# A decoder trunk's opening in two token halves, with the first norm's factor applied after the in-projection

## The chip, the cores and the metric

The kernel runs on one core of one Trainium2 chip. The metric is the device time of one execution in microseconds (us); the median of several executions is given. A core has five engines that run side by side, each through its own queue in order: TensorE (PE; matrix products and transposes, writes PSUM), VectorE (DVE), ScalarE (ACT), GpSimd (POOL) and SyncE (SP; here it only issues DMA transfers). SBUF is the working memory of 128 partitions, PSUM the memory that PE writes to, in eight banks of 512 float32 values per partition.

## What is computed

Two layers over 512 tokens with 1024 features, float32. The change touches the start of layer 0, a Mamba-2 mixer:

```python
def rms_norm(x, g):
    y = x * lax.rsqrt(jnp.mean(x * x, axis=-1, keepdims=True) + EPS)
    return y * g

def mamba2_mixer(x, ln_g, in_w, conv_w, conv_b, dt_bias, a_log, ...):
    zxbcdt = rms_norm(x, ln_g) @ in_w              # 1024 -> 2048 + 3072 + 32
    z, xbc, dt = split(zxbcdt)
    xbc = silu(causal_dwconv(xbc, conv_w, conv_b)) # width 4, per channel
    xs, bm, cm = split(xbc)                        # 2048, 4 * 128, 4 * 128
    dt = softplus(dt + dt_bias)
    a = dt * (-exp(a_log))
    y = ssd_chunked(xs * dt, a, bm, cm) + xs * d_skip
    y = grouped_rms_norm(y * silu(z))              # 4 groups
    return y @ out_w

x = x + mamba2_mixer(x, ...)
x = x + conv_ffn(x, ...)
# layer 1: differential attention with shared K/V, then conv_ffn
```

The norm's factor `rsqrt(mean(x^2) + EPS)` is one number per token, `g` one number per feature. Since the in-projection sums over features, the factor may be applied to x or to each token's result.

## The kernel before

Activations lie feature-major: a tile holds 128 features (partitions) by 512 tokens. x is eight such tiles `xT[k]` (the residual, tile `xTt`). Every product runs in split precision: an operand is rounded to the fast format (`xgh`, `wh`), the rest is kept as a second operand (`xgl`, `wl`), and three matmuls make one product (`mm3`: wh·xh, wh·xl, wl·xh). A block of 128 output features over 1024 input features is 24 matmuls of 512 columns.

Weights stream through `emit_chunk`: a DMA of 512 KB on SP's queue into one of three `raw` buffers, then `wh` on ACT (L148) and `wl` on DVE (L149). `plan` lists the chunks in the order of use, and `chunk(key)` emits up to two ahead. The tile framework allots buffers and writes semaphore waits; a scheduler places instructions on each engine's queue by its estimates, except those that `tc.keep_in_program_order` pins.

The opening (pool `ph0`): SP loads four blocks of 128 tokens by 1024 features (`xt`, L221), then the dt weights (128 KB) and the first weight chunks. ACT loads the convolution's parameters and the norm's `g` into `st1`. PE runs ten fp32 and eighteen fast warming matmuls (L257, L260) and turns `st1` into `c1`. For each token block ACT squares and sums (L267) and takes the root (L268), DVE inverts it (L269) and multiplies the block by it (L270) into `xr`. PE turns `xr` into eight PSUM banks, one per k (`xgt`, L274); each bank gets two readers, ACT's `xgh[k]` (times g, L277) and DVE's `xgl[k]` (L278). Then follow the dt product (16 matmuls, L435 and L439), block in32 (group 0's B), the four transposes of dt (L446), block in36 (group 0's C), and in16 to in19 (its x). From dt, DVE computes softplus and `A`, and PE the cumulated decays (`ps_dec`); two tables go to DRAM and come back broadcast as `m` and `er` (POOL's DMA queue, `fetch`).

Each of four groups then runs: two blocks for B and C and four for x, each with a width-4 convolution (`conv_block`: ACT takes the first tap from PSUM, DVE the other three, ACT applies SiLU); the chunked scan of four chunks (`scan`: `tokens`, `masked`, `states`, `outputs`), woven with the four z blocks (`z_blocks`: SiLU on ACT from PSUM); then `xs * z`, squares, their sum (`gacc`, L678), the group's norm factor (`tr_g`, `al_g`), and the out-projection of the group before, which adds to the residual `xT`.

The residual itself is not kept from the opening. In group 1 the same four blocks of x are loaded again (`x0` to `x3` in `plan`), turned by PE (32 transposes, L307) and copied to `xT` by ACT (L308), one block after each convolution block (`stream_in`).

Of the kernel before, what the change touches and what calls it, by code (L numbers as in the profile page):

```python
# [39 lines left out]
def trunk_kernel(ctx: ExitStack, tc, x, ssm_ln_g, ssm_in_w, ssm_conv_w, ssm_conv_b, ssm_dt_bias,  # L40
# [19 lines left out]
    def aux_bank(name):  # L60
        return pp.tile([P, T], F32, tag="aux", name=name)
# [60 lines left out]
    def emit_chunk():  # L122
# [5 lines left out]
        if key[0] == "x":  # L128
            raw = wrp.tile([P, D], F32, tag="raw", name="wr_" + key)
            sync.dma_start(raw, src)  # L130
            ready.append((key, raw, None))
            return
        nk, ncol = plan[i][2:4]
        n = nk * ncol
        raw = wrp.tile([P, 1024], F32, tag="raw", name="wr_" + key)
        wh = wp.tile([P, 1024], F32R, tag="wh", name="wh_" + key)
        wl = wp.tile([P, 1024], F32R, tag="wl", name="wl_" + key)
        sync.dma_start(raw[:, :n].rearrange("p (k c) -> p k c", k=nk), src)
        if len(plan[i]) > 4:

            for k in range(nk):
                ks = slice(k * ncol, (k + 1) * ncol)
                g = c2[:, plan[i][4] + k:plan[i][4] + k + 1]
                act.activation(wh[:, ks], raw[:, ks], AF.Copy, scale=g)
                dve.scalar_tensor_tensor(out=wl[:, ks], in0=raw[:, ks], scalar=g,
                                         in1=wh[:, ks].bitcast(F32), op0=ALU.mult, op1=ALU.subtract)
        else:
            act.activation(wh[:, :n], raw[:, :n], AF.Copy)  # L148
            dve.tensor_tensor(out=wl[:, :n], in0=raw[:, :n], in1=wh[:, :n].bitcast(F32), op=ALU.subtract)  # L149
        ready.append((key, wh[:, :n].rearrange("p (k c) -> p k c", k=nk),  # L150
                      wl[:, :n].rearrange("p (k c) -> p k c", k=nk)))

    def dt_chunk():

        key, src, nk, ncol = plan[0]
        state["next"] = state["use"] = 1
        raw = wrp.tile([P, 1024], F32, tag="raw", name="wr_dt")
        w = wp.tile([P, 1024], F32R, tag="wh", name="w_dt")
        rv = raw[:, :nk * ncol].rearrange("p (k c) -> p k c", k=nk)
        wv = w[:, :2 * nk * ncol].rearrange("p (k j c) -> p k j c", k=nk, j=2)  # L160
        sync.dma_start(rv, src)
        act.activation(wv[:, :, 0, :], rv, AF.Copy)
        dve.tensor_tensor(out=wv[:, :, 1, :], in0=rv, in1=wv[:, :, 0, :].bitcast(F32), op=ALU.subtract)
        return wv
# [26 lines left out]
    eps_c = cp.tile([P, 1], F32, name="eps_c")  # L191
    dve.memset(eps_c, EPS)
# [24 lines left out]
    with tc.tile_pool(name="ph0", bufs=1) as p0:  # L217
        xt = [p0.tile([P, D], F32, name="xt%d" % b) for b in range(NT)]
        xr = [p0.tile([P, D], F32, name="xr%d" % b) for b in range(NT)]
        for b in range(NT):  # L220
            sync.dma_start(xt[b], x[0, b * P:(b + 1) * P, :])  # L221
        st1 = p0.tile([P, P], F32, name="st1")
        act.preload_act_table_set("sqrt_and_others")
        act.dma_start(st1[0:96, :], ssm_conv_w.rearrange("o k (b p) -> (o k b) p", p=P))
        act.dma_start(st1[96:120, :], ssm_conv_b.rearrange("o (b p) -> (o b) p", p=P))
        act.dma_start(st1[120:128, :], ssm_ln_g.rearrange("o (b p) -> (o b) p", p=P))
        act.dma_start(dtb, ssm_dt_bias[0].partition_broadcast(P))
        act.dma_start(alog, ssm_a_log[0].partition_broadcast(P))
# [23 lines left out]
        wst = [p0.tile([P, P], F32R, name="wst%d" % i) for i in range(2)]  # L252
        wmv = p0.tile([P, T], F32R, name="wmv")
        for t in (*wst, wmv):
            dve.memset(t.bitcast(F32), 0.5)
# [6 lines left out]
        pe.transpose(ps[:, :P], st1, ident)  # L262
        dve.tensor_copy(c1, ps[:, :P])
        ss = p0.tile([P, NT], F32, name="ss")
        rs = p0.tile([P, NT], F32, name="rs")
        for b in range(NT):
            act.activation(xr[b], xt[b], AF.Square, accum_out=ss[:, b:b + 1])  # L267
            act.activation(rs[:, b:b + 1], ss[:, b:b + 1], AF.Sqrt, bias=eps_c, scale=1.0 / D)  # L268
            dve.reciprocal(rs[:, b:b + 1], rs[:, b:b + 1])  # L269
            dve.tensor_scalar(out=xr[b], in0=xt[b], scalar1=rs[:, b:b + 1], scalar2=None, op0=ALU.mult)  # L270
        pss = [(mm_bank if k % 2 else aux_bank)("xgt%d" % k) for k in range(KB)]
        for b in range(NT):
            for k in range(KB):
                pe.transpose(pss[k][:, b * P:(b + 1) * P], xr[b][:, k * P:(k + 1) * P], ident)  # L274
        for k in range(KB):
            g = c1[:, 120 + k:121 + k]
            act.activation(xgh[k], pss[k], AF.Copy, scale=g)  # L277
            dve.scalar_tensor_tensor(out=xgl[k], in0=pss[k], scalar=g, in1=xgh[k].bitcast(F32),  # L278
                                     op0=ALU.mult, op1=ALU.subtract)

    def params_a():
        dve.tensor_copy(st2[64:80, :].rearrange("p (j q) -> p j q", j=2),
                        d2[64:80, :].unsqueeze(2).to_broadcast([16, 2, 64]))
# [5 lines left out]
    def params_b():  # L289
# [4 lines left out]
        dve.tensor_tensor(out=lamv[:, 0], in0=lamv[:, 0], in1=lamv[:, 1], op=ALU.mult)  # L294
        dve.tensor_tensor(out=lamv[:, 1], in0=lamv[:, 2], in1=lamv[:, 3], op=ALU.mult)
        dve.reduce_sum(le, lamv[:, 0:2], axis=AX.X)
        act.activation(le, le, AF.Exp)
# [3 lines left out]

    def stream_in(b):
        xb, _ = chunk("x%d" % b)
        for q in range(2):
            ps = aux_bank("xt%d_%d" % (b, q))
            for k in range(4):
                pe.transpose(ps[:, k * P:(k + 1) * P], xb[:, (4 * q + k) * P:(4 * q + k + 1) * P], ident)  # L307
            act.activation(xTt[:, 4 * q:4 * q + 4, b * P:(b + 1) * P],  # L308
                           ps.rearrange("p (k t) -> p k t", k=4), AF.Copy)
# [47 lines left out]
    def along_tokens(r, name):  # L357

        ps = aux_bank("al_" + name)
        for b in range(NT):  # L360
            pe.transpose(ps[:, b * P:(b + 1) * P], r[:, 2 * b:2 * b + 1].to_broadcast([P, P]), ident)
        return ps
# [50 lines left out]
    with tc.tile_pool(name="ssm_y", bufs=1) as yp, tc.tile_pool(name="ssm", bufs=1) as sp:  # L413
        def in_block(key):
            wh, wl = chunk(key)
            ps = mm_bank("ps_" + key)
            for k in range(KB):
                mm3(ps, wh[:, k, :], wl[:, k, :], xgh[k], xgl[k], k == 0, k == KB - 1)
            return ps

        def conv_block(j, key, dst):
            ps = in_block(key)
            w = lambda t: c1[:, t * 24 + j:t * 24 + j + 1]
            tmp = sp.tile([P, T], F32, tag="ctmp", name="ctmp%d" % j, bufs=2)
            act.activation(tmp, ps, AF.Identity, bias=c1[:, 96 + j:97 + j], scale=w(3))
            for s in range(1, 4):
                dve.scalar_tensor_tensor(out=tmp[:, s:], in0=ps[:, :T - s], scalar=w(3 - s),
# [4 lines left out]
        wdt = dt_chunk()  # L432
        ps = aux_bank("ps_dt")
        for k in range(KB):
            both = lambda: pe.matmul(ps[:2 * NH, :], wdt[:, k].rearrange("p j c -> p (j c)"), xgh[k],  # L435
                                     start=(k == 0), stop=(k == KB - 1))
            if k < KB - 1:
                both()
            pe.matmul(ps[:NH, :], wdt[:, k, 0, :], xgl[k], start=False, stop=False)  # L439
            if k == KB - 1:  # L440
                both()
        dtT = sp.tile([P, T], F32, tag="ctmp", name="dtT", bufs=2)[:2 * NH, :]
        act.activation(dtT, ps[:2 * NH, :], AF.Copy)
# [11 lines left out]
        dve.tensor_tensor(out=v4(dt), in0=pv[:, :, 1, :], in1=v4(dt), op=ALU.add)  # L455
        dve.tensor_tensor(out=v4(dt), in0=v4(dt),
# [45 lines left out]
        class Chunk:  # L502
# [11 lines left out]
            def fetch(self):  # L514
# [4 lines left out]
                if self.c:  # L519
                    self.er = sp.tile([P, 4, P], F32, tag="er", name="er" + self.tag, bufs=3)  # L520
# [85 lines left out]
        def z_blocks(g, zs):  # L606
            for b in range(4):
                ps = in_block("in%d" % (4 * g + b))
                z = sp.tile([P, T], F32, tag="z", name="z%d_%d" % (g, b), bufs=4)
                act.activation(z, ps, AF.Silu)  # L610
# [38 lines left out]
        for g in range(NG):  # L649
# [6 lines left out]
            conv_block(16 + g, "in%d" % (32 + g), bT)  # L656
# [4 lines left out]
            for b in range(4):  # L661
# [3 lines left out]
                if g == 1:  # L665
                    stream_in(b)
# [343 lines left out]
```

## Time and profile before

| | us |
|---|---|
| median of 3 runs | 1390.85 (1390.69 to 1392.38) |
| the profiled execution | 1389.46 |
| its span, first to last instruction | 1387.6 |
| PE busy in the span | 1367.3 |
| DVE busy | 893.6 |
| ACT busy | 671.5 |
| granted clock of PE, mean | 0.999 |

The profile is of one execution. In a row of the timeline the first number is the start in us, the second the length, then engine, line, operation and tiles (out <- in), and in brackets the idle time of the engine just before it, with what ended it. A row of groups (by line) ends with busy time, the mean of one in ns, and idle time before. A row of waits names the waiting engine, tile and line, what it waited for, and the total, the number and the longest. A row of windows gives the stretch, its length, the busy time of each engine, PE's granted clock (1.00 is full), the DMA share and GB/s. A busy PE is not PE at its peak: matmuls of 512 columns last 0.39 us each but follow each other every 0.23 us.

### The profile page before, as it was taken

How to read it: one execution, taken by the hardware profiler on the slowest of the kernel's cores; microseconds unless marked ns; L12 is line 12 of the kernel's file. 1: busy time of each engine (PE TensorE's matmuls, PEld its weight loads, DVE VectorE, ACT ScalarE, POOL GpSimd, SP SyncE). 2: the span in 40 equal slices, each digit the busy share in tenths (PEclk: the TensorE clock that was granted, in tenths of full speed). 3: DMA queues.
4: the chain of work that ended last, by engine and by line, in shares of the span. 5: the costliest groups of instructions: out<-in, count | busy, mean ns of one | idle time of the engine just before them, and what ended most of it. 6: DMA issues, size and time to landing. Idle time of an engine off the chain costs nothing.

```text
span 1387.6 us, 17001 instructions
## 1 busy us (share of the span) xinstructions
PE 1367.3 (99%) x6480; PEld 1105.0 (80%) x6480; DVE 893.6 (64%) x1481; ACT 671.5 (48%) x1108; POOL 93.2 (7%) x117
## 2 busy tenths in 40 slices
PE   8999999999999999999999999999999999999998
PEld 6777787787878888888888786786778888888886
DVE  6687767768677775357754546748687774367741
ACT  6785644742344443134433557757654442144431
POOL 4330300300020000000001000000020000000000
PEclk9999999999999999999999999999999999999999
DMA  6655433432223333233323422221133332333322
GB/s 183 163 148 148 129 91 107 129 103 65 80 88 107 91 97 101 91 104 95 93 82 112 114 90 68 66 87 39 48 103 93 93 105 91 99 99 91 99 92 69
DMA packets 188422, 137.18 MB, mean 99 GB/s; under 512 B 6852, under 2 KB 177268, under 8 KB 188340
## 3 DMA queue, kind: packets, MB, share of 16 engines
q1 hardware_dynamic: 181312, 122.93, 30.1%
q0 software_dynamic: 4400, 12.01, 2.9%
q10 hardware_dynamic: 2628, 1.15, 0.3%
q8 instruction: 51, 0.84, 0.2%
q14 instruction: 31, 0.25, 0.1%
HBM read 133.82 MB, written 2.25 MB: 98 GB/s over the span
## 4 chain that ended last, share of the span: by engine, by line
PE 76%; DVE 5%; ACT 4%; issue 1%; DMA 0%; POOL 0%; POOLq 0%; ACTq 0%
PE ps_u L175 6%; PE ps_u L177 6%; PE ps_d L176 6%; PE ps_d L177 6%; PE ps_u L176 6%; PE ps_d L175 6%; PE ps_g L176 6%; PE ps_g L177 6%; PE ps_g L175 5%; PE ps_in L175 2%; PE ps_in L177 2%; PE ps_in L176 2%; PE ps_o L176 2%; PE ps_o L177 2%; PE ps_o L175 1%
## 5 line engine op out<-in xcount | busy, mean ns | idle before, releaser
L176 PE MATMUL ps_g<-xgl,wh_g 128*128 128x512 f32 x352 | 137.2, 390 | 1.5 <-DVE xgl L319 1.5
L175 PE MATMUL ps_d<-hh,wh_d 128*128 128x512 f32 x352 | 137.5, 391 | 0.0
L177 PE MATMUL ps_d<-hh,wl_d 128*128 128x512 f32 x352 | 137.2, 390 | 0.0
L175 PE MATMUL ps_u<-xgh,wh_u 128*128 128x512 f32 x352 | 137.1, 390 | 0.0
L176 PE MATMUL ps_u<-xgl,wh_u 128*128 128x512 f32 x352 | 137.1, 390 | 0.0
L175 PE MATMUL ps_g<-xgh,wh_g 128*128 128x512 f32 x352 | 137.0, 389 | 0.1
L176 PE MATMUL ps_d<-hl,wh_d 128*128 128x512 f32 x352 | 137.0, 389 | 0.0
L177 PE MATMUL ps_u<-xgh,wl_u 128*128 128x512 f32 x352 | 136.9, 389 | 0.0
L177 PE MATMUL ps_g<-xgh,wl_g 128*128 128x512 f32 x352 | 136.9, 389 | 0.0
L175 PE MATMUL ps_in<-xgh,wh_in 128*128 128x512 f32 x320 | 126.9, 397 | 0.0
L177 PE MATMUL ps_in<-xgh,wl_in 128*128 128x512 f32 x320 | 126.3, 395 | 0.0
L176 PE MATMUL ps_in<-xgl,wh_in 128*128 128x512 f32 x320 | 125.9, 393 | 0.0
L149 DVE TENSOR_TENSOR wl_d<-wr_d,wh_d 128x1024 fp32r<-128x1024 f32 (+1 forms) x48 | 54.5, 1136 | 91.7 <-ACT wh_d L148 91.5
L148 ACT ACTIVATE wh_d<-wr_d 128x1024 fp32r<-128x1024 f32 (+1 forms) x48 | 47.5, 990 | 129.5 <-PE ps_d L176 115.3
L724 ACT ACTIVATE hh<-vg 128x512 fp32r<-128x512 f32 x44 | 27.8, 631 | 114.9 <-DVE vg L723 114.9
L707 DVE TENSOR_TENSOR uu<-ps_u,nr_f 128x512 f32<-128x512 f32 x44 | 30.4, 692 | 79.6 <-PE ps_u L177 79.6
L176 PEld LDWEIGHTS ps_g<-xgl,wh_g 128*128 128x128 f32 x352 | 66.1, 188 | 16.0 <-DVE xgl L319 2.3
L175 PEld LDWEIGHTS ps_g<-xgh,wh_g 128*128 128x128 f32 x352 | 66.1, 188 | 14.2 <-ACT xgh L318 0.5
L177 PEld LDWEIGHTS ps_u<-xgh,wl_u 128*128 128x128 f32 x352 | 66.1, 188 | 13.7
L176 PEld LDWEIGHTS ps_u<-xgl,wh_u 128*128 128x128 f32 x352 | 66.1, 188 | 13.7
L176 PEld LDWEIGHTS ps_d<-hl,wh_d 128*128 128x128 f32 x352 | 66.1, 188 | 13.6
L177 PEld LDWEIGHTS ps_d<-hh,wl_d 128*128 128x128 f32 x352 | 66.1, 188 | 13.5
(315 smaller groups left out, 2950.4 us busy)
## 6 DMA issues: line engine op xcount, KB each, us to landing
wr_g<-in_ffn_up_w_dram SPq DMA_DIRECT2D x44, 512.0 KB, 3.8
wr_u<-in_ffn_up_w_dram SPq DMA_DIRECT2D x44, 512.0 KB, 3.9
wr_in<-in_ssm_in_w_dram SPq DMA_DIRECT2D x40, 512.0 KB, 3.9
wr_d<-in_ffn_down_w_dram SPq DMA_DIRECT2D x40, 512.0 KB, 3.5
m<-cumd POOLq DMA_DIRECT2D x16, 512.0 KB, 5.1
wr_out<-in_ssm_out_w_dram SPq DMA_DIRECT2D x16, 512.0 KB, 3.4
wr_k<-in_kv_w_dram SPq DMA_DIRECT2D x8, 512.0 KB, 3.9
wr_q<-in_q_w_dram SPq DMA_DIRECT2D x8, 512.0 KB, 4.1
```

The lines of the kernel that those rows point to most:

```text
L148: act.activation(wh[:, :n], raw[:, :n], AF.Copy)
L149: dve.tensor_tensor(out=wl[:, :n], in0=raw[:, :n], in1=wh[:, :n].bitcast(F32), op=ALU.subtract)
L175: pe.matmul(ps, wh, xh, start=start, stop=False)
L176: pe.matmul(ps, wh, xl, start=False, stop=False)
L177: pe.matmul(ps, wl, xh, start=False, stop=stop)
L707: dve.tensor_tensor(out=u, in0=ps, in1=r, op=ALU.mult)
L724: act.activation(h, ga, AF.Copy)
```

## The change

- The opening works in halves of 256 tokens. x is turned as it is, without the norm's factor. A PSUM bank (`xgt0_q`, `xgt1_q`) holds two k slices of one half.
- SP issues x0, x1, the dt weights, in32's weights, x2, x3. ACT loads only `g` (`st0`, turned into `g1`) and the convolution's weights; POOL loads its bias, `dtb` and `alog`.
- For half 0 and then half 1: ACT and DVE make `xgh` and `xgl` (times g) for 256 tokens, PE runs the dt product and block in32 over those columns. The order on the engines is pinned.
- The residual is copied from the same PSUM banks (`keep`), two of half 0's on DVE early, the rest later on DVE and ACT; the second load of x, its turns and copies in group 1 are gone.
- Sums of squares go to `rs`, for x0 and x2, x3 on ACT and x1 on DVE. The inverse root is computed on DVE by `rsqrt` (twelve small steps). PE spreads it along tokens (`al_x`), ACT copies it to `nr_x`.
- Each block of the in-projection is multiplied by `nr_x` on DVE, before the convolution (`u`) and before z's SiLU; dt is multiplied by `rs`.
- The table of functions that ACT loads first is another; the eighteen fast warming matmuls are gone; `er` has two buffers in place of three.

```diff
@@ plan
-            if g == 1:
-                plan.append(("x%d" % b, x[0, b * P:(b + 1) * P, :]))
@@ opening
-        for b in range(NT):
+        for b in range(2):
             sync.dma_start(xt[b], x[0, b * P:(b + 1) * P, :])
-        act.preload_act_table_set("sqrt_and_others")
+        act.dma_start(st0, ssm_ln_g.rearrange("o (b p) -> (o b) p", p=P))
+        act.preload_act_table_set("natural_log_exp_and_others")
...
-        for n in (T, T // 2, P):
-            for i in range(6):
-                pe.matmul(warm[:, :n], wst[i % 2], wmv[:, :n], start=True, stop=True)
...
+        def turn(h, b, q):
+            for k in range(2):
+                pin(pe.transpose(pv[h][q][:, k, (b % 2) * P:(b % 2 + 1) * P],
+                                 xt[b][:, (2 * q + k) * P:(2 * q + k + 1) * P], ident))
+
+        def high(h, m):
+            pin(act.activation(xgh[m][:, half[h]], pv[h][m // 2][:, m % 2], AF.Copy, scale=g1[:, m:m + 1]))
+
+        def low(h, m):
+            pin(dve.scalar_tensor_tensor(out=xgl[m][:, half[h]], in0=pv[h][m // 2][:, m % 2],
+                                         scalar=g1[:, m:m + 1], in1=xgh[m][:, half[h]].bitcast(F32),
+                                         op0=ALU.mult, op1=ALU.subtract))
+
+        def keep(h, q, on):
+            o = xTt[:, 2 * q:2 * q + 2, half[h]]
+            pin(act.activation(o, pv[h][q], AF.Copy) if on is act else dve.tensor_copy(o, pv[h][q]))
...
+        half = (slice(0, 256), slice(256, T))
+        pst = [[aux_bank("xgt0_%d" % q) for q in range(4)]]
+        pv = [[p.rearrange("p (k t) -> p k t", k=2) for p in pst[0]]]
+        pin(act.activation(sq[0], xt[0], AF.Square, accum_out=rs[:, 0:1]))
+        pin(dve.tensor_tensor_reduce(sq[1], xt[1], xt[1], 1.0, 0.0, ALU.mult, ALU.add, rs[:, 1:2]))
+        wdt = dt_chunk()
+        for b in range(2):
+            for q in range(4):
+                turn(0, b, q)
+        for m in range(KB):
+            high(0, m)
+            low(0, m)
+            if m in (1, 3):
+                keep(0, m // 2, dve)
+            if m == 3:
+                emit_chunk(pin)
+                for b in range(2, NT):
+                    sync.dma_start(xt[b], x[0, b * P:(b + 1) * P, :])
+        wb0 = ready[0][1:]
+        ps_dt, ps_b0 = mm_bank("ps_dt"), mm_bank("ps_in32")
+        dt_part(half[0])
+        pst.append([(mm_bank if q < 2 else aux_bank)("xgt1_%d" % q) for q in range(4)])
+        pv.append([p.rearrange("p (k t) -> p k t", k=2) for p in pst[1]])
+        turn(1, 2, 0)
+        turn(1, 2, 1)
+        b0_part(half[0])
+        turn(1, 2, 2)
+        turn(1, 2, 3)
+        for q in range(4):
+            turn(1, 3, q)
+        for m in range(KB):
+            high(1, m)
+            low(1, m)
+        dt_part(half[1])
+        b0_part(half[1])
+        emit_chunk(pin)
+        for q in range(2, 4):
+            keep(0, q, dve)
+        for q in range(4):
+            keep(1, q, act)
+        emit_chunk(pin)
+        chunk("in32")
+        for b in (2, 3):
+            pin(act.activation(sq[0], xt[b], AF.Square, accum_out=rs[:, b:b + 1]))
@@ conv_block, z_blocks
+            u = sp.tile([P, T], F32, tag="u", name="u%d" % j, bufs=2)
+            dve.tensor_tensor(out=u, in0=ps, in1=rr, op=ALU.mult)
...
-            act.activation(tmp, ps, AF.Identity, bias=c1[:, 96 + j:97 + j], scale=w(3))
+            act.activation(tmp, u, AF.Identity, bias=c1[:, 96 + j:97 + j], scale=w(3))
...
-                act.activation(z, ps, AF.Silu)
+                dve.tensor_tensor(out=z, in0=ps, in1=rr, op=ALU.mult)
+                act.activation(z, z, AF.Silu)
@@ the norm's factor, dt
+        rsqrt(rs, sp, "x", [P, NT], D)
+        rr = bp.tile([P, T], F32, tag="nr", name="nr_x")
+        act.activation(rr, along_tokens(rs, "x", 1), AF.Copy)
...
+        dve.tensor_tensor(out=v4(dt), in0=v4(dt), in1=rs.unsqueeze(2).to_broadcast([P, NT, NH]), op=ALU.mult)
@@ er
-                    self.er = sp.tile([P, 4, P], F32, tag="er", name="er" + self.tag, bufs=3)
+                    self.er = sp.tile([P, 4, P], F32, tag="er", name="er" + self.tag, bufs=2)
```

`dt_part(ts)` and `b0_part(ts)` are the 16 matmuls of the dt product and the 24 of block in32 over the columns `ts`; in `b0_part` the low weights come last.

More of the change, by code (lines that the diff above doesn't have):

```diff
@@ L127, in emit_chunk @@
         key, src = plan[i][:2]
[L128 to L132, printed above, removed]
         nk, ncol = plan[i][2:4]
@@ L263, in trunk_kernel @@
[L263 to L270, printed above, removed]
@@ L271, in trunk_kernel @@
-        pss = [(mm_bank if k % 2 else aux_bank)("xgt%d" % k) for k in range(KB)]
-        for b in range(NT):
-            for k in range(KB):
[L274 to L279, printed above, removed]
+        pe.transpose(ps[:, :KB], st0, ident[:KB, :KB])
@@ new lines, in trunk_kernel @@
+        dve.tensor_copy(g1, ps[:, :KB])
+        sq = [p0.tile([P, D], F32, name="xsq%d" % i) for i in range(2)]
+        def turn(h, b, q):
[8 more added lines that the diff above has]
+                                         op0=ALU.mult, op1=ALU.subtract))
@@ new lines, in keep, with dt_part @@
+        def keep(h, q, on):
+            o = xTt[:, 2 * q:2 * q + 2, half[h]]
+            pin(act.activation(o, pv[h][q], AF.Copy) if on is act else dve.tensor_copy(o, pv[h][q]))
+        def dt_part(ts):
+            for k in range(KB):
+                both = lambda: pin(pe.matmul(ps_dt[:2 * NH, ts], wdt[:, k].rearrange("p j c -> p (j c)"),
+                                             xgh[k][:, ts], start=(k == 0), stop=(k == KB - 1)))
+                if k < KB - 1:
+                    both()
+                pin(pe.matmul(ps_dt[:NH, ts], wdt[:, k, 0, :], xgl[k][:, ts], start=False, stop=False))
+                if k == KB - 1:
+                    both()
@@ new lines, in b0_part @@
+        def b0_part(ts):
+            for k in range(KB):
+                pin(pe.matmul(ps_b0[:, ts], wb0[0][:, k, :], xgh[k][:, ts], start=k == 0, stop=False))
+                pin(pe.matmul(ps_b0[:, ts], wb0[0][:, k, :], xgl[k][:, ts], start=False, stop=False))
+            for k in range(KB):
+                pin(pe.matmul(ps_b0[:, ts], wb0[1][:, k, :], xgh[k][:, ts], start=False, stop=k == KB - 1))
+        half = (slice(0, 256), slice(256, T))
+        pst = [[aux_bank("xgt0_%d" % q) for q in range(4)]]
@@ L413, in trunk_kernel, with in_part @@
     with tc.tile_pool(name="ssm_y", bufs=1) as yp, tc.tile_pool(name="ssm", bufs=1) as sp:
+        def in_part(ps, wh, wl, ts):
+            for k in range(KB):
+                mm3(ps[:, ts], wh[:, k, :], wl[:, k, :], xgh[k][:, ts], xgl[k][:, ts], k == 0, k == KB - 1)
         def in_block(key):
```

85 lines of the change are left out of this document (33 added, 52 removed).

## Prediction

> **What bounds the kernel now.** I read the page's part 1 first, then the list of waits of PE, then the opening as a timeline, then windows of busy time in the stretch where the change also works.
>
> ```profile
> span 1387.6 us, 17001 instructions
> PE 1367.3 (99%) x6480; PEld 1105.0 (80%) x6480; DVE 893.6 (64%) x1481; ACT 671.5 (48%) x1108; POOL 93.2 (7%) x117
> PE tr_g L351 <- DVE gacc L678: 2.5, 2, 1.3
> PE xgt L274 <- DVE xr L270: 1.6, 2, 1.2
> PE ps_dt L435 <- DVE xgl L278: 1.6, 1, 1.6
> PE cb L539 <- ACT xT L308: 1.2, 1, 1.2
> ```
>
> PE is busy 1367.3 of 1387.6 us; all its idle time is 20.3 us. So a change can win PE work that it takes out, one of these waits, or opening time in which PE runs things that lead nowhere. This kernel's end is PE's end: I follow when PE finishes a block, before and after.
>
> ```profile
> 0.81 4.58 SPq L221 DMA_DIRECT2D xt<-in_x_dram  x4
> 5.07 1.06 ACT L267 ACTIVATE xr<-xt 128x1024 f32<-128x1024 f32 x1 [2.98 <-DMA xt<-in_x_dram]
> 6.03 0.19 ACT L267 ACTIVATION_READ_ACCUMULATOR xr<-xt 128x1 f32 x1
> 6.27 1.06 ACT L267 ACTIVATE xr<-xt 128x1024 f32<-128x1024 f32 x1
> 10.80 1.06 ACT L267 ACTIVATE xr<-xt 128x1024 f32<-128x1024 f32 x1 [1.65 <-DMA xt<-in_x_dram]
> 11.86 0.40 ACT L162 ACTIVATE w_dt<-wr_dt 128x256 fp32r<-128x256 f32 x1
> 13.26 1.06 ACT L148 ACTIVATE wh_in<-wr_in 128x1024 fp32r<-128x1024 f32 x1 [0.81 <-DMA wr_in<-in_ssm_in_w_dram]
> 14.22 4.72 ACT L277 ACTIVATE xgh<-xgt,c 128x512 fp32r<-128x512 f32 x8
> 16.29 0.45 PE L435 MATMUL ps_dt<-xgh,w_dt 128*64 128x512 f32 x1 [1.56 <-DVE xgl L278]
> 26.15 0.39 PE L175 MATMUL ps_in<-xgh,wh_in 128*128 128x512 f32 x1
> 31.59 0.39 PE L175 MATMUL ps_in<-xgh,wh_in 128*128 128x512 f32 x1
> ```
>
> This is the opening: first number the start, second the length, in brackets the idle time and who ended it. The first token block of x is there at 5.07, the fourth at 10.80; only then are the eight conversions xgh possible (14.22), the dt product starts at 16.29, and PE then runs without a gap: dt, in32, four small transposes, from 26.15 in36, from 31.59 in16. So 31.59 is the mark: everything up to in36, with dt turned, is done.
>
> **The change, part by part.** First what is taken out. In group 1 x is read again, turned by PE and copied by ACT.
>
> ```profile
> L307 PE MATMUL xt<-ident,wr_x x32: 270/272/273, 109.2 to 129.0; 128*128 128x128 f32 x32
> L308 ACT ACTIVATE xT<-xt x8: 584/592/601, 111.2 to 131.5; 128x512 f32<-128x512 f32 x8
> 128.25 1.04 PE L307 MATMUL xt<-ident,wr_x 128*128 128x128 f32 x8
> 129.13 0.49 PE L548 MATMUL xs<-ident,xs 128*128 128x128 f32 x3
> 131.65 0.49 PE L539 MATMUL cb<-cT,bT 128*128 128x128 f32 x2 [1.24 <-ACT xT L308]
> ```
>
> The 32 turns come in groups of eight, and one group holds PE from 128.25 to 129.13, 0.88 us; four make 3.5. The copies sit on ACT, and the last holds a PSUM bank for which PE waits 1.24. Four loads leave SP's queue, no load is late there. Gain 3.5 + 1.24 = 4.75 us. If something else is late at 131.65, up to 1.24 of it stays: 3.5 to 4.75. I take 4.75. Also gone are the 18 warming matmuls, the fp32 factor multiplies xr and square roots of the opening; the first were in front of PE's wait and hide nothing, the others are replaced below.
>
> Now the new opening. SP issues x0, x1, the dt weights, in32, x2, x3, and POOL takes over three small loads from ACT's queue ahead of its own, whose results are used far later. x0 and x1 are there at 5.07 and 6.27 (rows above), turned by 7.3. The dt weights, queued behind all of x, were used at 11.86; now two blocks of x fewer stand before them, at 1.2 us each and some weight traffic moved back: 7.2 to 8.2. I start the first conversion at 7.95. Its length for 256 columns is not in the trace; neighbours are
>
> ```profile
> L277 ACT ACTIVATE xgh<-xgt,c 128x512 fp32r<-128x512 f32 x8 | 4.7, 699 | 0.0
> L278 DVE SCALAR_TENSOR_TENSOR xgl<-xgt,c,xgh 128x512 fp32r<-128x512 f32 x8 | 5.4, 742 | 0.0
> L149 DVE TENSOR_TENSOR wl_in<-wr_in,wh_in 128x1024 fp32r<-128x1024 f32 x5 | 6.1, 1220 | 1.7 <-ACT wh_in L148 1.6
> L458 DVE SCALAR_TENSOR_TENSOR sp_p<-dt 128x128 f32<-128x128 f32 x1 | 0.3, 291 | 0.0
> 359.03 0.17 DVE L326 TENSOR_SCALAR rsm_g<-tr_g 128x8 f32<-128x8 f32 x1
> 359.24 0.17 DVE L327 TENSOR_SCALAR tr_g<-rsm_g 128x8 int32<-128x8 int32 x1
> ```
>
> ACT: 0.40 for 256 columns from SBUF with a constant factor (w_dt), 0.70 for 512 from PSUM with a column factor, so 0.40 to 0.60; I take 0.50. DVE: 0.29 at 128, 0.74 at 512, on the line between them 0.44. I add 0.05 for each hop.
>
> What decides is the bank. A half of 256 tokens puts two k slices into one PSUM bank, and in the new program's waits the engines take the bank in turns: xgh of the odd slice waits for xgl of the even one. Before, each k had a bank of its own, so ACT ran ahead. A bank now costs 0.50 + 0.05 + 0.44 + 0.05, twice, = 2.08; the even xgh of the next bank overlaps, so each further one adds 1.53. Four banks: 2.08 + 3 x 1.53 = 6.7 us per half, where the full width took DVE's 5.4. In the first half DVE also copies two banks to the residual (0.6 each, as ACT's L308) and makes in32's low part (1.22, waiting for ACT's 1.06): I add 2.4, and the half ends at 7.95 + 6.7 + 2.4 = 17.0.
>
> PE is in order: behind dt's first half come four turns (0.44), in32's first half (24 matmuls of 256 columns at a pitch of half of 0.23, 2.9), then the turns that the second half's first conversion needs (0.7). So that starts at 17.3 + 0.44 + 2.9 + 0.7 = 21.4, ends at 28.1; dt's last matmul 28.4, in32's second half 31.3, and in36 starts at 31.4 against 26.15.
>
> Before in36 can end, PE must turn the norm's factor rs (four transposes), and the squares of x2 and x3 were put late on ACT: after the last xgh at 27.6 come wh_in36 1.06, four residual copies 2.4, wh_in16 1.06, square 1.25, wh_in17 1.06, square 1.25 = 35.7. DVE's twelve small steps of the inverse root have a pitch of 0.20 (rows L326, L327): 38.1. PE has done in36's first 23 matmuls at 31.4 + 5.2 = 36.6 and waits 1.5. Four transposes, four for dt, one matmul: in16 starts at 39.2. Against 31.59 that is +7.6. Its bounds: conversions at the short ends (0.40, 0.36) and dt weights at 7.2 shorten the halves by 2 and the start by 0.8, +4.8; no turn-taking at the bank, down to +3; long ends (0.60, 0.52), +9.5. Behind it stand in16, in17, in18 on PE, 17 us of work that covers the chain from dt to A, as in36 to in18 did before; I cost it at nothing, 0.5 if it is late.
>
> [...] By the Trainium skill, "PSUM — Partial Sum Buffer", section "PSUM bank collisions raise a hardware error", engines must not be in one bank at once, and guards have to keep them apart; by it the opening costs the 7.6, without such guards its bound of 3; the row of eight xgh in 4.72 us without a pause shows ACT free of DVE with separate banks, and no run here shows two slices in one.
>
> Last, each of 40 in-projection blocks gets a DVE multiply by the factor, because the factor is no longer in x.
>
> ```profile
> L707 DVE TENSOR_TENSOR ug<-ps_g,nr_f x44: 682/686/692, 411.6 to 1318.7; 128x512 f32<-128x512 f32 x44
> core 0: us, PE busy (x) PEld busy (x) DVE busy (x) ACT busy (x) POOL busy (x), PEclk, DMA share, GB/s
> 137.60:159.70 22.10, 22.10 (x154) 16.67 (x153) 21.07 (x39) 12.70 (x25) 6.62 (x11) 1.00 0.41 130
> 159.70:173.20 13.50, 12.31 (x56) 9.89 (x54) 6.33 (x8) 11.65 (x16) 5.24 (x5) 1.00 0.40 120
> 170.03 0.69 DVE L671 TENSOR_TENSOR xs<-xs,z 128x512 f32<-128x512 f32 x1 [1.22 <-ACT z L610]
> ```
>
> The same multiply takes 0.69 in the feed-forward part: 28 us of DVE in all. Group 1's scan (137.6 to 159.7) has DVE at 21.07 of 22.10; behind it, to 173.2, it is busy 6.33 of 13.5. So two of four multiplies fall in a full stretch, two in a loose one. In the first, PE's blocks of in-projection stand between the scan's matmuls and cover DVE's delay, 0 to 1.4 us a group; at the end z comes 0.7 later, before tr_g, for which PE waited 2.5 in two groups. In the new order groups 1 and 2 have four and six more matmuls in front of tr_g, 0.9 and 1.4 us. I take 0.7 for all four groups, from 0 to 5.5 (four times 1.4). One buffer of er fewer delays its fetch to after outputs(1); two scan steps, about 9 us, cover it.
>
> Sum: 7.6 - 4.75 + 0.7 = +3.5. On the profiled execution: 1389.46 (span 1387.6 and 1.9 around it) + 3.5 = 1393.0. The median of the runs shown, 1390.85, lies 1.4 above that execution, so I say 1394.
>
> ```profile
> 5.00:8.64 3.64, 3.24 (x23) 2.79 (x21) 0.97 (x3) 3.52 (x7) 2.37 (x5) 1.00 0.91 273
> 8.64:16.29 7.65, 4.25 (x33) 3.44 (x33) 5.21 (x12) 5.16 (x12) 5.88 (x11) 1.00 1.05 238
> 175.50:179.00 3.50, 3.50 (x10) 2.68 (x10) 1.85 (x9) 2.42 (x9) 0.00 (x0) 0.51 0.58 160
> ```
>
> The clock: PE, busy 4.25 of 7.65 us in the old opening, kept the full clock (1.00), but at 175.5 it had 0.51 for 3.4 us, after a stretch with the wait for tr_g. The new opening is sparser (some 2 us of 9). A cold 3.4 us over full work costs 1.7; twice, 3.4. Much of it would fall into PE's wait of 1.5 for rs, so +1 to +2; the old window may also vanish, -1.7. I take zero. [...]
>
> **The rivals.** (1) The opening costs nothing: x0 arrives 5.7 us before x3, and if halves overlap, in16 starts at 31.6 or a bit sooner; then only the removal counts, 1390.85 - 4.75 = 1386. For it: that early landing. Against it: PE's order, which holds the second half behind in32's first. (2) Conversions short, little turn-taking: opening +4, sum 4 - 4.75 + 0.4, 1390.5: no change. (3) Slower, by DVE: in the scans the multiplies run into the 21.07 of 22.10, 1.4 per group reach PE and tr_g is 0.7 later in each: 4 x 2.1 = 8.4, with the opening at +6: 1390.85 + 6 - 4.75 + 8.4 = 1400. It decides from where DVE has no idle time left before the scan's last step. Against it: the loose stretch.
>
> **How the numbers follow.** Forecast 0.50, (1) 0.18, (2) 0.20, (3) 0.12. A change under 0.2%, 2.8 us, can't be told from none: faster means below 1388.1, slower above 1393.6. Faster: (1) and a little of (2), 0.20. Slower: (3) and most of the forecast, 0.52; the rest 0.28. The range reaches from (1) to just under (3), 1386 to 1399; the forecast's own is 1391 to 1397.
>
> **What would show it.** Right: in16's first matmul at 38 to 40, second-half conversions from about 21, xgh of odd slices with idle time ended by DVE's xgl, PE's wait for DVE at the factor's transposes; no L307 and no wait of cb in group 1. Wrong: in16 before 35 (rival 1 or 2), DVE-ended waits of PE in the scans above 5 us in sum (rival 3), or a granted clock of 0.5 for more than one window before 40 us.

## The result and the profile after

The changed kernel takes 1396.92 us (median of 4 runs, 1394.13 to 1398.54) against 1390.77 (1389.08 to 1392.38): +6.2 us, ratio 1.0045 with a 95% interval of 1.0027 to 1.0062. The profiled execution has a span of 1396.8 us, 9.2 more than before; it is the longest of the four, so places are read from it and totals from medians.

The page's head and its list of PE's waits (total, times, longest), for the changed kernel:

```profile
span 1396.8 us, 17046 instructions
PE 1373.6 (98%) x6475; PEld 1111.0 (80%) x6475; DVE 916.4 (66%) x1537; ACT 668.1 (48%) x1104; POOL 94.2 (7%) x120
PE tr_g L398 <- DVE gacc L729: 5.1, 4, 3.4
PE ps_dt L278 <- DVE xgl L264: 4.0, 11, 1.0
PE ps_dt L274 <- ACT xgh L261: 1.5, 6, 0.5
```

PE is busy 6.3 us longer with five instructions fewer, and idles 23.2 us in place of 20.3. The wait for the residual's copies (`cb`) is gone; waits for the conversions (5.5 in sum) and a long one for `tr_g` have come. More busy time for no more work means a slower clock. Windows of the changed kernel (stretch, length, busy time of each engine, PE's granted clock, DMA share, GB/s) show it in the opening and once in group 2:

```profile
7.90:14.10 6.20, 3.20 (x15) 1.40 (x13) 4.57 (x8) 3.10 (x7) 4.03 (x8) 1.00 1.11 340
14.13:20.90 6.77, 6.06 (x26) 4.98 (x27) 1.36 (x3) 1.28 (x3) 5.93 (x12) 0.50 0.55 139
20.95:27.75 6.80, 5.54 (x34) 3.55 (x33) 2.67 (x7) 2.99 (x7) 0.52 (x2) 1.00 0.03 8
27.85:34.60 6.75, 6.18 (x28) 5.70 (x29) 4.47 (x6) 6.37 (x11) 0.00 (x0) 0.50 0.28 78
273.60:280.40 6.80, 6.74 (x20) 5.71 (x21) 3.60 (x13) 1.90 (x7) 0.00 (x0) 0.50 0.28 78
```

Three stretches of 6.8 us run at half clock; before there was one of 3.4 us, at 175.5. Full work loses half of such a stretch.

Where the time went is read from the first matmul of a block, found from its place in the order of the in-projection's matmuls; in33, in34 and in35 open groups 1, 2 and 3, and "up" is the first matmul of layer 0's feed-forward part. The table gives the start of in16 and the lengths of the steps behind it, in us, for all kernels that ran (the rows below those two are explained in the next section):

| kernel | in16 starts | in16 to in33 | in33 to in34 (group 1) | in34 to in35 (group 2) | in35 to up (group 3) | median of runs | ratio to before, 95% |
|---|---|---|---|---|---|---|---|
| before | 31.59 | 59.31 | 101.51 | 92.90 | 113.54 | 1390.77 | |
| changed | 41.34 | 59.31 | 94.36 | 97.99 | 114.31 | 1396.92 | 1.0027 to 1.0062 |
| e1, third er | 40.24 | 58.45 | 100.44 | 95.93 | 114.27 | 1401.05 | 1.0071 to 1.0117 |
| e2, alternating banks | 34.02 | 59.35 | 93.62 | 95.77 | 114.30 | 1390.26 | 0.9989 to 1.0015 |
| e3, filled | 38.02 | 58.66 | 93.69 | 95.74 | 114.28 | 1393.74 | 1.0017 to 1.0046 |
| e4, x again | 41.23 | 59.52 | 100.84 | 95.66 | 114.27 | 1403.08 | 1.0077 to 1.0116 |
| e5, e2 with late masks | 33.92 | 59.15 | 104.94 | 94.44 | 113.64 | 1399.32 | 1.0050 to 1.0083 |
| e6, e2 without z's factor | 33.99 | 59.45 | 94.49 | 92.61 | 113.69 | 1385.28 | 0.9954 to 0.9980 |
| e7, changed without z's factor | 41.21 | 59.16 | 94.56 | 92.36 | 113.74 | 1391.85 | 1.0006 to 1.0026 |
| e8, e2 with z on POOL | 34.56 | 59.80 | 105.18 | 94.21 | 115.35 | 1397.19 | 1.0036 to 1.0078 |
| e9, e2 with two masks kept | 34.37 | 58.53 | 95.57 | 93.07 | 116.14 | 1388.35 | 0.9971 to 0.9999 |
| e10, e9 and filled | 33.60 | 59.34 | 95.20 | 95.82 | 114.65 | 1388.66 | 0.9972 to 0.9996 |

So the change lost 9.75 us in the opening, nothing from in16 to in33, won 7.15 in group 1, lost 5.1 in group 2 and 0.8 in group 3: +8.5. Of the last 0.7 up to 9.2, PE's wait for `xgl` behind up is 1.0 shorter (0.5 in place of 1.5), and a window of half clock late in the program (1031 us) costs 1.7. Which windows fall differs between executions of one kernel: over the executions of the kernel before, PE's mean granted clock goes from 0.994 to 1.000, and a window of 3.4 us is worth 0.001 of it. So each step of a single profile can carry a window's 1.7 us of chance. The kernel before was run again beside each batch of experiments, with medians from 1389.25 to 1391.13; where medians of two batches are compared, the ratios are the safer measure.

The opening in the timeline of the changed kernel, rows of ACT, DVE and PE (start, length, engine, line, tiles, and in brackets the idle time before with what ended it):

```profile
7.91 0.47 ACT L261 ACTIVATE xgh<-xgt,g 128x256 fp32r<-128x256 f32 x1 [0.48 <-DVE w_dt L158]
8.93 0.84 ACT L261 ACTIVATE xgh<-xgt,g 128x256 fp32r<-128x256 f32 x2 [0.55 <-DVE xgl L264]
16.03 0.48 DVE L264 SCALAR_TENSOR_TENSOR xgl<-xgt,g,xgh 128x256 fp32r<-128x256 f32 x1 [0.55 <-ACT xgh L261]
22.94 0.47 ACT L261 ACTIVATE xgh<-xgt,g 128x256 fp32r<-128x256 f32 x1 [6.95 <-PE xgt L257]
23.97 0.84 ACT L261 ACTIVATE xgh<-xgt,g 128x256 fp32r<-128x256 f32 x2 [0.55 <-DVE xgl L264]
28.73 0.48 DVE L264 SCALAR_TENSOR_TENSOR xgl<-xgt,g,xgh 128x256 fp32r<-128x256 f32 x1 [0.54 <-ACT xgh L261]
34.76 0.48 PE L170 MATMUL ps_in<-xgh,wh_in 128*128 128x512 f32 x1
38.54 0.17 DVE L381 SCALAR_TENSOR_TENSOR rs<-rst_x,rs 128x4 f32<-128x4 f32 x1
40.09 0.60 PE L408 MATMUL al_x<-ident,rs 128*128 128x128 f32 x4
41.34 0.39 PE L170 MATMUL ps_in<-xgh,wh_in 128*128 128x512 f32 x1
```

The brackets are the story: ACT waits for DVE's `xgl`, DVE for ACT's `xgh`, and between 16.5 and 22.9 the conversions wait for PE's turns. The factor `rs` is ready at 38.71, PE comes for it only at 40.09.

### The profile page after: what moved, and what is told of

Read it like the earlier page. It is cut to its first block, busy times and chain, and to the rows that moved or that the text cites. A ratio compares the mean times of both kernels' runs of the same rounds, so it can differ in the third digit from the quotient of the medians.

```text
span 1396.8 us, 17046 instructions
## 1 busy us (share of the span) xinstructions
PE 1373.6 (98%) x6475; PEld 1111.0 (80%) x6475; DVE 916.4 (66%) x1537; ACT 668.1 (48%) x1104; POOL 94.2 (7%) x120
## 4 chain that ended last, share of the span: by engine, by line
PE 83%; DVE 7%; ACT 6%; issue 2%; DMA 1%; POOL 1%; POOLq 0%; SPq 0%; ACTq 0%; DVEq 0%
PE ps_u L170 6%; PE ps_u L171 6%; PE ps_u L172 6%; PE ps_d L170 6%; PE ps_d L171 6%; PE ps_d L172 6%; PE ps_g L170 6%; PE ps_g L171 6%; PE ps_g L172 6%; PE ps_in L172 4%; PE ps_in L171 4%; PE ps_in L170 4%; PE ps_o L171 2%; PE ps_o L172 2%; PE ps_o L170 2%
## 5 line engine op out<-in xcount | busy, mean ns | idle before, releaser
L170 PE MATMUL ps_in<-xgh,wh_in 128*128 128x512 f32 x312 | 123.3, 395 | 0.0
L172 PE MATMUL ps_in<-xgh,wl_in 128*128 128x512 f32 x312 | 122.6, 394 | 0.0
L170 PEld LDWEIGHTS ps_u<-xgh,wh_u 128*128 128x128 f32 x352 | 66.5, 189 | 13.8
L172 PEld LDWEIGHTS ps_g<-xgh,wl_g 128*128 128x128 f32 x352 | 66.1, 188 | 13.8
```

The costliest lines, as they stand in the source:

```text
L170: pe.matmul(ps, wh, xh, start=start, stop=False)
L172: pe.matmul(ps, wl, xh, start=False, stop=stop)
```

## The experiments

My theory after the result had four parts: the conversions take turns at a bank; the sparse dt stretches drop the clock; the removal of the second load of x is worth its sum; and group 2 is lost by the fetch of `er`, with one buffer fewer. The rival to the last was the DVE multiply of z.

**e1: three buffers for er, nothing else.**

```diff
-                    self.er = sp.tile([P, 4, P], F32, tag="er", name="er" + self.tag, bufs=2)
+                    self.er = sp.tile([P, 4, P], F32, tag="er", name="er" + self.tag, bufs=3)
```

> The changed kernel with three buffers for er again, nothing else. My theory: in the changed kernel er_g_3 is fetched only after outputs(1), its fetch stands on POOL's queue ahead of the masks of the next group's m, ACT waits for those masks (3.35 us at 258.9) and with it z's SiLU, so that PE waits 3.4 us for tr_g in group 2 and the clock drops behind it. Then with three buffers PE's wait for tr_g in group 2 falls to 1.3 or less, the step from in11 to in35 falls from 35.4 us to 30 to 32, and the time is 2 to 5 us lower than the changed kernel's: 1392 to 1395. Rival (the DVE multiplies by the factor delay z): the wait stays near 3 us, the time within 1 us of the changed kernel's, 1396 to 1398.

Measured: 1401.05 us, slower by 4. Group 2 is 95.93, in the range of the other variants, with a wait of 2.7; the same trouble now stands in group 1 (100.44). ACT's row there:

```profile
166.26 0.99 ACT L582 ACTIVATE m<-m,ncum 128x128 f32<-128x128 f32 x3 [3.45 <-POOL m L577]
PE tr_g L398 <- DVE gacc L729: 3.4, 1, 3.4
```

The buffer isn't the cause; my theory of `er` fell. ACT's wait for POOL's mask while z's SiLU is queued behind it is seen again, now with PE's long wait in group 1. That wait of ACT alone doesn't decide: in group 1 of the changed kernel it is 3.87 us, and PE waits only 0.7 for `tr_g`.

**e2: the slices converted so that two banks are in use.**

```diff
+        alt = (0, 2, 1, 3, 4, 6, 5, 7)
...
-        for m in range(KB):
+        for m in alt:
             high(0, m)
             low(0, m)
...
-        for m in range(KB):
+        for m in alt:
             high(1, m)
             low(1, m)
...
         def dt_part(ts):
-            for k in range(KB):
+            for k in alt:
```

> The changed kernel with the slices converted in the order 0, 2, 1, 3, 4, 6, 5, 7, so that ACT and DVE stand on different PSUM banks. My theory (they take a bank in turns): the second half's eight conversions take about 4.2 us in place of 6.2 (xgh0 at 22.94 to the end of xgl7 at 29.2), the first half ends 1.5 to 2.2 us sooner, and in16's first matmul comes at 37 to 38.5 in place of 41.34; time 1393 to 1394. Rival (DVE sets the pace of the conversions anyway, or PE waits for rs instead): in16 at 40.5 or later, time within 1 us of the changed kernel's.

Measured: 1390.26 us, 6.7 below the changed kernel (6.0 by the ratios) and level with the kernel before; in16 at 34.02, more than expected. The groups of conversions over the opening, first of the changed kernel (busy us, mean ns, idle before and what ended it):

```profile
L261 ACT ACTIVATE xgh<-xgt,g 128x256 fp32r<-128x256 f32 x16 | 7.0, 472 | 13.4 <-PE xgt L257 7.0 <-DVE xgl L264 6.0 <-DVE w_dt L158 0.5
L264 DVE SCALAR_TENSOR_TENSOR xgl<-xgt,g,xgh 128x256 fp32r<-128x256 f32 x16 | 7.4, 480 | 11.8 <-ACT xgh L261 11.8
```

then of this kernel, with its conversions' first and last rows in the second half and in16's first matmul:

```profile
L261 ACT ACTIVATE xgh<-xgt,g 128x256 fp32r<-128x256 f32 x16 | 6.7, 471 | 8.0 <-PE xgt L257 6.1 <-DVE xgl L264 1.9
L264 DVE SCALAR_TENSOR_TENSOR xgl<-xgt,g,xgh 128x256 fp32r<-128x256 f32 x16 | 7.0, 478 | 6.7 <-ACT xgh L261 6.3
19.62 0.84 ACT L261 ACTIVATE xgh<-xgt,g 128x256 fp32r<-128x256 f32 x2 [6.13 <-PE xgt L257]
21.15 2.69 DVE L264 SCALAR_TENSOR_TENSOR xgl<-xgt,g,xgh 128x256 fp32r<-128x256 f32 x6
13.30:16.50 3.20, 3.13 (x15) 2.57 (x14) 0.70 (x2) 0.18 (x1) 1.72 (x4) 0.50 1.19 293
16.70:34.00 17.30, 16.46 (x104) 13.09 (x104) 10.57 (x27) 12.18 (x22) 4.58 (x10) 1.00 0.38 104
34.02 0.39 PE L170 MATMUL ps_in<-xgh,wh_in 128*128 128x512 f32 x1
```

Same durations, but ACT's idle time that `xgl` ended is 1.9 in place of 6.0, and the second half's conversions go from 19.62 to 23.84, 4.2 us in place of 6.3. The denser opening also keeps the clock from 16.7 on: of four windows of half clock one is left.

**e3: the gaps filled.** 84 matmuls into columns that block in32 overwrites.

```diff
+                for _ in range(3 if k < KB - 1 else 0):
+                    pin(pe.matmul(ps_b0[:2 * NH, half[1]], wdt[:, 0].rearrange("p j c -> p (j c)"),
+                                  wdt.rearrange("p k j c -> p (k j c)")[:, :256], start=True, stop=True))
                 pin(pe.matmul(ps_dt[:NH, ts], wdt[:, k, 0, :], xgl[k][:, ts], start=False, stop=False))
+                (the same three again)
```

> The changed kernel with 84 filling matmuls of 256 columns between the dt product's matmuls in both halves, into columns that are overwritten later. My theory (the sparse dt stretches drop the clock for two windows of 3.4 us each): granted clock 1.00 from 8 to 40 us, in32's first half in 2.9 us in place of 4.4, its second in 2.9 in place of 5.0, then PE waits up to 1.2 us for rs, and in16 starts at 37.5 to 39 in place of 41.34: time 2 to 4 us lower than the changed kernel's. Rival (the clock does not hang on these gaps): windows at half clock as before, in16 at 41.3 to 42.5, time the same or up to 1 us higher.

Measured: 1393.74 us, in16 at 38.02: as expected. The median is 3.2 below the changed kernel's; by the ratios it is 2.0, and their intervals overlap. The same stretches as above:

```profile
7.90:14.10 6.20, 5.34 (x42) 4.23 (x41) 4.73 (x9) 3.10 (x7) 4.08 (x9) 1.00 1.08 337
14.13:20.90 6.77, 6.77 (x60) 6.46 (x59) 1.36 (x3) 1.18 (x4) 5.55 (x12) 1.00 0.63 153
27.85:34.60 6.75, 6.75 (x44) 6.12 (x43) 5.51 (x13) 6.00 (x10) 0.00 (x0) 1.00 0.56 155
35.79 0.65 PE L414 MATMUL al_x<-ident,rs 128*128 128x128 f32 x4 [0.32 <-DVE rs L387]
```

Useless work on PE makes the opening 3.3 us shorter: the clock stays whole, and PE now waits for the factor, as the prediction had it, only 0.32 rather than 1.5.

**e4: the second load of x put back**, `stream_in` and its entries in the plan as before the change, `keep` left out.

```diff
-            if m in (1, 3):
-                keep(0, m // 2, dve)
...
-        for q in range(2, 4):
-            keep(0, q, dve)
-        for q in range(4):
-            keep(1, q, act)
...
+                if g == 1:
+                    stream_in(b)
```

> The changed kernel with the second load, turn and copy of x in group 1 put back and the residual copies of the opening left out. If the removal was worth what I summed, group 1's four x blocks (in20 to in4) take 3.5 us longer again and PE's wait for the copies returns: 4 to 5 us from in33 to in7 more than in the changed kernel; the opening is 0 to 1 us shorter without the copies (1.2 of it on DVE in the first half); time 3 to 5 us higher, 1400 to 1402. Rival (the turns were hidden, the gain went elsewhere): within 1.5 us of the changed kernel's.

Measured: 1403.08 us, 6.2 above the changed kernel (7.2 by the ratios). From in33 to the last z block of group 1 the step is 3.7 us longer (its first matmul at 169.29 - 100.75 = 68.5 against 165.47 - 100.65 = 64.8): the turns alone, PE's wait for the copies did not return. The rest of the 6.5 us in group 1 comes behind: a longer wait for `tr_g` (1.9 in place of 0.7) and a window of half clock at 184.8. The opening gained only 0.1: the copies were hidden. Group 2 takes 95.66, 2.3 less than in the changed kernel, near the 95.74 to 95.93 of e1, e2 and e3: of the changed kernel's 97.99, one window of half clock, 1.7, is missing in each of them.

**e5: all masks kept in the program's order on ACT** (on e2).

```diff
-                    act.activation(v, v, AF.Exp, bias=ncum[:, col:col + 1])
+                    pin(act.activation(v, v, AF.Exp, bias=ncum[:, col:col + 1]))
```

> The kernel with alternating banks, and the exponentials of the next group's masks kept in the order of the program on ACT, behind this group's z, where the scheduler had put them between z's SiLUs. My theory (group 2's longer wait for tr_g comes from ACT, which waits 3 us for POOL's mask and changes its table of functions twice between z_1 and z_3): PE's wait for tr_g in group 2 falls from 2.5 to 1 or less, no window at half clock behind it, the step from in34 to in35 falls from 95.8 to 92 to 93.5 us, and the time is 2 to 4 us below the kernel with alternating banks: 1386 to 1388. Rival (the DVE multiply of z alone): the wait stays at 2 or more, the time the same. A third way: the masks come late for the next group's scan and PE waits there, 1390 or more.

Measured: 1399.32 us, the third way. Group 2 is 94.44 in place of 95.77, but group 1 takes 104.94: the masks now stand in front of the convolutions' SiLU, PE waits, and 10.2 us at half clock follow (from 142.7).

```profile
PE xs L598 <- ACT xs L484: 3.9, 1, 3.9
138.21 4.21 ACT L583 ACTIVATE m<-m,ncum 128x128 f32<-128x128 f32 x14
142.43 1.28 ACT L484 ACT_TABLE_LOAD   x1
143.73 0.63 ACT L484 ACTIVATE xs<-ctmp 128x512 f32<-128x512 f32 x1
```

**e6 and e7: z not multiplied by the factor**, on e2 and on the changed kernel.

```diff
-                dve.tensor_tensor(out=z, in0=ps, in1=rr, op=ALU.mult)
-                act.activation(z, z, AF.Silu)
+                act.activation(z, ps, AF.Silu)
```

> The kernel with alternating banks, with the multiply of z by the norm's factor left out (16 multiplies of 0.69 us; the output is then not the reference's). If the multiply itself is what lengthens group 2's end, PE's wait for tr_g falls from 2.5 to 1 or less and the step from in34 to in35 to 92 to 93.5. If it is the masks between z's SiLUs on ACT, which stay there, the wait falls by at most 0.7 per multiply on the chain, to 1.5 to 2.5, and the step stays above 94.5. Time 1389 to 1390 by the second, 1387 to 1388 by the first.

> The changed kernel itself with only the multiply of z by the factor left out (16 multiplies; the output is not the reference's), the banks as in the change. If the pieces add up: the opening unchanged (in16 at 41.3), the step from in34 to in35 92.6 to 93.5 in place of 98.0, time 4 to 6 us below the changed kernel's: 1391 to 1393. If the multiply matters only beside a fast opening, the step stays above 95 and the time within 2 us of the changed kernel's.

Measured: 1385.28 us, 5.0 below e2, and 1391.85 us, 5.1 below the changed kernel (4.9 and 4.0 by the ratios): the pieces add up, with a slow opening and a fast one. Group 2 is back at 92.61 and 92.36 (before: 92.90). PE's wait for `tr_g` in that stretch, of the changed kernel, e2, e6 and e7 in this order:

```profile
PE tr_g L398 <- DVE gacc L729: 3.4, 1, 3.4
```
```profile
PE tr_g L399 <- DVE gacc L730: 2.5, 1, 2.5
```
```profile
PE tr_g L399 <- DVE gacc L729: 0.9, 1, 0.9
```
```profile
PE tr_g L398 <- DVE gacc L728: 0.6, 1, 0.6
```

So the multiply of z brings the price in group 2: 1.6 to 2.8 us of wait, and behind a wait of 2.5 or more a window or two of half clock, which do not follow the shorter waits of e6 and e7. The length of the wait doesn't settle that: waits of 1.2 (the kernel before, 175.5), 1.9 (e4, 184.8) and 1.1 (e9, 358.4) were followed by a window, one of 1.8 (e5, group 1) was not. Group 2's end in the changed kernel shows how 0.69 us become that much:

```profile
258.89 2.16 ACT L582 ACTIVATE m<-m,ncum 128x128 f32<-128x128 f32 x7 [3.35 <-POOL m L577]
263.61 0.63 ACT L660 ACTIVATE z<-z 128x512 f32<-128x512 f32 x1
265.29 0.68 DVE L659 TENSOR_TENSOR z<-ps_in,nr_x 128x512 f32<-128x512 f32 x1
268.64 1.28 ACT L660 ACT_TABLE_LOAD   x1
269.93 0.63 ACT L660 ACTIVATE z<-z 128x512 f32<-128x512 f32 x1
273.66 1.63 PE L398 MATMUL tr_g<-ones,gacc 128*128 128x2 f32 x7 [3.40 <-DVE gacc L729]
```

The masks of the next group stand between the z on ACT, with their own table of functions. The last z is multiplied by 265.97 and goes through SiLU only at 269.93. Masks stand there without the multiply too, but the scheduler then chose another order, here in e7:

```profile
251.16 3.92 ACT L582 ACTIVATE m<-m,ncum 128x128 f32<-128x128 f32 x13
257.68 1.06 ACT L143 ACTIVATE wh_out<-wr_out 128x1024 fp32r<-128x1024 f32 x1 [2.60 <-PE ps_in L171]
260.05 0.60 ACT L659 ACTIVATE z<-ps_in 128x512 f32<-128x512 f32 x1
```

Between the second and the third z of group 2 ACT computes 22 masks in the changed kernel and in e2 and waits 3.35 and 3.06 for POOL's mask; in e6 and e7 it computes 13 and does not wait for one. So these two runs took out the multiply and this order together. How much of the price is the multiply's own 0.69 us and how much the order is not shown by them.

**e8: three of four z multiplied on POOL** (on e2).

```diff
+                if b < 3:
+                    act.activation(z, ps, AF.Copy)
+                    pool.tensor_tensor(out=z, in0=z, in1=rr, op=ALU.mult)
+                else:
+                    dve.tensor_tensor(out=z, in0=ps, in1=rr, op=ALU.mult)
```

> The kernel with alternating banks, where three of each group's four z blocks are copied from PSUM by ACT and multiplied by the factor on POOL, the last one on DVE as before; the result is the same. If DVE's time in the scans is the price (2.1 us less of it per group), PE's wait for tr_g in group 2 falls from 2.5 to 1 or less and the time is 2 to 5 us below the kernel with alternating banks and below the kernel before: 1385 to 1388. If the length of z's own chain is the price (multiply before SiLU, longer on POOL), the wait stays at 2.5 or more and the time at 1390 or above.

Measured: 1397.19 us. In group 2 PE's wait for `tr_g` fell from 2.5 to 1.2 and the step from 95.77 to 94.21, but group 1 takes 11.6 us more (105.18 against 93.62): PE waits 5.3 for `tr_g` there, and 6.8 us at half clock follow (from 177.8). The edit also puts twelve copies on ACT, with another order there, so it doesn't part DVE's time from the length of z's chain; it shows that this way of easing DVE costs more than it wins.

```profile
L662 POOL TENSOR_TENSOR z<-z,nr_x x12: 1264/1293/1849, 74.4 to 359.1; 128x512 f32<-128x512 f32 x12
PE tr_g L399 <- DVE gacc L734: 5.3, 1, 5.3
```

**e9: only the masks of chunks 2 and 3 kept in order** (on e2), **and e10: filled in the first half besides.**

```diff
-                    act.activation(v, v, AF.Exp, bias=ncum[:, col:col + 1])
+                    (pin if self.c >= 2 else lambda i: i)(act.activation(v, v, AF.Exp, bias=ncum[:, col:col + 1]))
```

> The kernel with alternating banks, where only the masks of chunks 2 and 3 keep the program's order on ACT (they may no longer run ahead between the z blocks of the group before); those of chunks 0 and 1 may. If the masks between z's SiLUs add to the price of the multiply, PE's wait for tr_g in group 2 falls from 2.5 to 1.5 or less, the step from in34 to in35 from 95.8 to 92.5 to 94, and the time is 1 to 4 us below the kernel with alternating banks: 1386 to 1389. If only the multiply counts, or the masks then hold up the convolutions as in the run with all of them kept, 1390 or more.

> The same with two filling matmuls beside each of the first half's dt matmuls. If the one window at half clock that is left in the opening (13.2 to 16.6 us) costs what it covers, the granted clock is 1.00 from 8 to 40 us and in16 starts at 33 to 33.8 in place of 34.0: time 0 to 1 us below the kernel with two masks kept. If it covers only sparse work, in16 is at 34.0 or a little later and the time the same.

Measured: 1388.35 and 1388.66 us, ratios to before 0.9985 (0.9971 to 0.9999) and 0.9984 (0.9972 to 0.9996): a little below the kernel before. Against e2 (1.0002, 0.9989 to 1.0015) the intervals overlap, so a gain over e2 is not shown. In e9 group 2 takes 93.07, the wait is 1.1, and ACT goes from one z to the next without a mask between:

```profile
PE tr_g L399 <- DVE gacc L730: 1.1, 1, 1.1
252.81 0.64 ACT L661 ACTIVATE z<-z 128x512 f32<-128x512 f32 x1
258.24 0.62 ACT L661 ACTIVATE z<-z 128x512 f32<-128x512 f32 x1
```

Group 3 took 1.8 us more there than in e2, with a window of half clock at 358.4, and group 1 2.0 more: what group 2 won was lost in its neighbours. In e10 in16 comes at 33.60, 0.8 sooner than in e9, but its median is the same: that gain is below what the runs can tell. In its group 2 no mask stands between the last z either, and yet PE waits 2.6 and the step is 95.82:

```profile
PE tr_g L405 <- DVE gacc L736: 2.6, 1, 2.6
257.86 1.96 POOL L584 TENSOR_SCALAR_AFFINE_SELECT m<-m 128x1024 f32<-128x1024 f32 x1 [4.06 <-DMA m<-cumd]
260.83 1.30 POOL L736 TENSOR_TENSOR gacc<-gsq,gsq 128x512 f32<-128x512 f32 x1
```

Here POOL's mask waits for its transfer and stands in front of POOL's part of the sum of squares, which comes 1.3 us later than in e9. So ACT's order is one way in which the wait gets long, and not the only one.

## Why the prediction was right or wrong

The direction was right and the time lay in the range, 1396.92 against 1394 and 1386 to 1399. Two terms of the sum were far off all the same, the clock and the multiply. The steps:

- **The opening, +7.6 forecast, +9.75 measured.** The first conversion (7.95, measured 7.91), a half's turns (6.7, measured 6.3) and the end of the first half (17.0, measured 16.5) came as summed, and e2 confirms the turn-taking. Mis-sized was the clock, taken as zero: block in32 took 4.4 and 5.0 us per half in place of 2.9, 3.6 more; PE's wait for `rs`, summed as 1.5, was used up by that. 3.6 - 1.5 is the 2.1 that is missing. e3 gives the drop's price as 3.3 us at in16. The forecast had reasoned that most of such a drop would fall into PE's wait for `rs`; the drop was four windows and outgrew that wait.
- **The conversions' idle time costs twice.** The lower bound without turn-taking, +3, is near e2's in16 at +2.4, but for another reason in part: of the 7.3 us that e2 wins there, the fill alone (e3) wins 3.3, and the two are not independent, because a denser opening is also a warmer one.
- **The removal, -4.75 forecast.** Group 1 is 7.15 shorter. The turns' 3.5 are confirmed (3.7 in e4). The wait for the copies did not return in e4, where ACT's order is another. Most of the other 2.4 is a window of half clock (1.7) behind group 1 that before had and the changed kernel's profile has not.
- **The factor's multiply, +0.7 forecast, 4 to 5 measured** (e6, e7). This step was furthest off. The bound for it, 5.5, held. The place was named, a later z in front of `tr_g`, but the price was taken as the multiply's own 0.7, and loose time on DVE was to absorb the rest. What counts is the chain after the last z (multiply, table, SiLU, square, sum), which ends in PE's wait for `tr_g`, with the order of ACT and POOL around it and the clock behind it. How the price divides among these stays open. Between e7 and the changed kernel groups 0 and 1 show no loss and group 3 0.6; group 2 has 5.6.
- **The third buffer of er, at nothing.** Giving the buffer back made the kernel slower (e1), so the change did not lose there; what the buffer alone is worth stays open, since e1's order on ACT and POOL is another too.
- **Rivals.** (1) and (2) needed a cheap opening; e2 shows that it was within reach, by the order of eight slices. (3) named the right instruction and also a later `tr_g`, but put two thirds of its price into the scans and spread it over all groups; it came in one.
- **The signs.** Of those for being right, the turn-taking and the missing wait of `cb` came; in16 at 38 to 40 and PE's wait at the factor's transposes did not (41.34, and PE came 1.4 us after `rs` was ready). Of those for being wrong one came: half clock for more than one window before 40 us.

The sum's parts were off by about +2.1, -2.4 and +4. That the total stayed in the range is in part luck: the surplus of the removal, mostly a window of half clock that the changed kernel's profile happened not to have, stood against the other two.

## What to carry to other kernels

When two engines read the same PSUM bank, let consecutive steps alternate between banks: the order of the steps alone was worth 6 to 7 us here, with what it did to the clock. A stretch in which PE waits can be paid again in the clock behind it, so a stall of a few us should be priced with the window that may follow. A cheap step put in front of an activation is priced by the chain behind it and by the order that the scheduler then chooses around it, not by the engine's share of busy time.

## What the runs showed of the hardware

Half clock came in windows of 3.4 us or two or three times that (10.2 in e5 and e7): behind PE's wait of 3.4 us for `tr_g` in group 2, but also in the opening, where no gap was over 1.0 us long and PE counted as busy 3.20 of 6.20 us. With 5.34 of 6.20 busy (e3) the clock stayed whole. In the Trainium skill, "TensorE: Matmul & The Clock Gate", Part 1, the table of the two states puts half clock behind an idle window of about 3.4 us; by the row of 7.90 to 14.10 a thin stretch without such a window is enough. How thin is not told by PE's busy time: the second drop stands behind 20.95 to 27.75 with 5.54 of 6.80 busy, while the old opening kept full clock with 4.25 of 7.65. On POOL a multiply of 128x512 took 1.29 us (median of 12), against 0.69 on DVE.
